# Layer 2's output projection in four parts, one of them by seven products of halves, and half of a gate's row sums moved to layer 1

## The chip, the cores and the metric

One core of a Trainium2 chip runs the whole program. Its engines work side by side, each through its own queue in program order: TensorE (PE) multiplies, VectorE (DVE) and ScalarE (ACT) work on elements, GpSimd (POOL) does a few small operations, and SyncE (SP) issues most of the transfers from HBM. An instruction waits until what it needs is there, and everything behind it in the same queue waits with it. The metric is the device time of one execution in microseconds (us); less is better.

## The reference

A two-layer trunk over 512 tokens of width 2048, in float32. Layer 1 mixes tokens by retention, layer 2 by latent attention; each ends in an output projection whose result is scaled by a gate and added to its input:

```python
x = x + gate1 * ((silu(g) * retention(q, k, v)) @ w_ret_out)      # layer 1
x = x + gate2 * ((silu(g) * attention(q, k, v)) @ w_mla_out)      # layer 2
out = rmsnorm(x, final_g)
```

The gates (and the shifts and scales of the two norms) are row sums of a large matrix with the conditioning vector: `mod = ada_w @ silu(c)`. `w_mla_out` is 2048 x 2048. This is a condensed form of the reference.

## The kernel before

**Products.** Float32 accuracy comes from three passes: each operand is split into a high and a low part (ACT casts, DVE subtracts), and PE adds hi x hi, hi x lo and lo x hi. So one block of a projection, 128 rows of input by 128 columns of weights over 512 tokens, takes three products of 128x512. A function `split` does the cast and the subtraction. For a weight tile of 128x1024 they are one instruction each.

**Seven products.** Some projections of the kernel are computed by halves (a form of Strassen's method, `seven_rows_steps`): rows of inputs and columns of weights are cut in two, sums and differences are formed, and seven products of halves replace eight. They run in two phases. Phase one has four steps of four products into banks x, s, z, y of PSUM; phase two has three products a step, which add onto x, y and s. Between the phases ACT copies x to m1 and s to m5 (L991), and DVE adds them into y (L1056) and s (L1058). Layer 2's gate is computed so (tiles `g_00e` to `g_13o`; "e" and "o" are the even and odd row halves, "10" to "13" the units of phase two).

**Layer 1's output projection** (L1486) runs in three blocks of sixteen steps and a last block. A step has one unit of weights: `o_n_r_u_r` as loaded, `o_n_r_u_p` its two split parts, 24 products of 128x512. Beside it run the heads of retention: statistics on DVE (L1320), a root on POOL (L131), `nmr` on DVE (L1326), the normalisation on ACT (L1332). Between them stand row sums for later modulations: a load of 512 KB by SP (L1165) into one of two buffers, and a sum on DVE (L1170) over 128x1024. How many sums each step gets is a list of step numbers given to `light`; the loads come one step ahead.

**Layer 2's output projection** takes the columns of `w_mla_out` in three rounds. Rounds 0 and 1 take a quarter each (512 columns; 8 units of 24 products, four banks). The last round takes the third and fourth quarter together (L2450): 16 units of 1024 columns, one row block each, into eight banks. Of them the last five units (`N_ENDS`) are held back and multiplied bank by bank in two halves of the tokens, so that outputs can start early. Inputs are loaded once, but split again in each round (`o2_parts`). In this stage also run the loads and sums for the second half of layer 2's gate (`gate_load`, `gate_sum`, L2157). An output (`o2_out`) is a DVE operation that scales by the gate and adds the residual (L2417), a square on ACT (L2422), a multiplication on ACT (L2423) and an addition of the squares on DVE (L2427).

**What sets the order.** The program is written out in order, and a scheduler places instructions of the engines within it; `behind(...)` and `queued(...)` pin a piece of code behind what was last placed on the named engines. Raw weights have three buffers (`raw`), split ones three pairs.

Of the kernel before, what the change touches and what calls it, by code (L numbers as in the profile page):

```python
# [16 lines left out]
P = 128  # L17
# [32 lines left out]
def hybrid_trunk_kernel(  # L50
# [1101 lines left out]
    row_pieces = [(0, 2, 0), (0, 2, 1), (1, 0, 0), (1, 0, 1), (1, 1, 0), (1, 1, 1)]  # L1152
# [397 lines left out]
    light(block, (0, 0, 2, 2, 4, 5, 6, 6))  # L1550
# [589 lines left out]
    gate_sums = [base.tile([P, 2, 8], F32, tag="mod_c", bufs=2, name=f"gate_sums{i}") for i in range(2)]  # L2140

    def gate_load(part, n):

        j, b = n // 8, n % 8
        if b == 0:
            half = gate_c_half[j] = big(f"c_gate{part}{j}", F32)
# [4 lines left out]
        aw = l2_tile("bw", 2, f"mod_gate_{part}{b}{j}", (P, 2, T))  # L2151
        r0 = 2 * D + (8 * part + b) * P
        nc.sync.dma_start(aw, ada_t[1, r0 : r0 + P, j * 1024 : (j + 1) * 1024].rearrange("p (a n) -> p a n", a=2))
        return aw, part, j, b, gate_c_half[j]

    def gate_sum(aw, part, j, b, c_half):
        DVE.scalar_tensor_tensor(  # L2157
            out=aw, in0=aw, scalar=1.0, in1=c_half, op0=ALU.mult, op1=ALU.mult,
            accum_out=gate_sums[part][:, j, b : b + 1],
        )  # L2160
        if (j, b) == (1, 7):
            use_modulation(1, 2, part, gate_sums[part])

    def attention_step(pr):
# [5 lines left out]
        with behind(S_):  # L2170
            sums = [gate_load(0, 2 * nx + i) for i in range(2)]
# [189 lines left out]
    x2 = [k4(f"x2_{j}", F32) for j in range(KD // 2)]  # L2361
    ss2 = l2p.tile([P, T], F32, tag="o2", bufs=2, name="x2_ss")
    o2_in, o2_res = {}, {}
    N_ENDS = 5

    gate_pending, gate_n = [], [0, 0]

    def o2_hooks(i):
        l2_hooks.get(i, lambda: None)()
        with behind(V_):  # L2370
            while gate_pending:
                gate_sum(*gate_pending.pop())
        with behind(S_):
            for _ in range(min(1, 16 - gate_n[0]) if 4 < i and i > gate_n[1] else 0):
                gate_pending.insert(0, gate_load(1, gate_n[0]))
                gate_n[0] += 1
        gate_n[1] = i

    def o2_parts(r, u):
        if u not in o2_in:  # L2380
            o2_in[u] = big(f"o2_in{u}", F32)
            nc.sync.dma_start(o2_in[u], o2_d[u * 2 * P : (u + 1) * 2 * P, :].rearrange("(k p) n -> p k n", p=P))
        own = big if (r, u) == (2, KD // 2 - 1) else k4b
        hi, lo = own(f"o2_h{r}_{u}"), own(f"o2_l{r}_{u}")
        split(o2_in[u], hi, lo)
        return hi, lo

    o2_split = {(0, 0): queued(o2_parts, 0, 0)}
# [4 lines left out]
    def o2_unit(r, u, kn, cn, where=None):  # L2393
        halved = kn == 1 and u >= KD - N_ENDS
        with ExitStack() as stack:
            for ins in o2_first if (r, u) in ((0, 1), (0, 2)) else ():
                stack.enter_context(tc.issue_after(ins))
            wt = load_w(
                [(whole, rows(w_mla_out, u, kn, r * T, cn))], kn, cn, f"o2_w{r}_{u}", where=where, halved=halved
            )  # L2400
        k = r, u * kn // 2
        if k not in o2_split:
            o2_split[k] = o2_parts(*k)
        return wt, o2_split[k]

    def o2_moving(w, kt, cols=slice(0, T)):
        return tuple(a[:, kt % 2, cols] for a in w[1])

    def o2_out(kt, ps, half=None):

        cols = slice(0, T) if half is None else slice(half * H, (half + 1) * H)
        if kt not in o2_res:
            tag, bufs = ("sg", 3) if kt >= 13 else ("pp", 5)
            o2_res[kt] = l2p.tile([P, T], F32, tag=tag, bufs=bufs, name=f"o2_xr{kt}")
            nc.sync.dma_start(o2_res[kt], x1_d[kt * P : (kt + 1) * P, :])
# [200 lines left out]
```

## Time and profile before

| | us |
|---|---|
| median of three runs (2119.68 to 2120.03) | 2119.76 |
| span of the profiled execution | 2118.4 |
| layer 1's output projection, PE | 997.2 to 1430 |
| layer 2's output projection, rounds 0 and 1, PE | 1920.7 to 2017.0 |
| the last round, PE (L2450) | 2017.0 to 2105.7 |

The profiled execution was not timed by itself; its span is 1.4 us under the median of the runs. The row of a timeline gives the start and the length of a piece of work in us, the engine, the line, the operation, what is written and read, and in brackets how long the engine had been idle before it and what ended that. Rows of the chain give start, length, engine and line. Names are without buffer numbers, so `o_p` is the split weights of any unit. Rows of matmuls give their full latency; the pace is the distance from start to start.

### The profile page before, as it was taken

How to read it: one execution, taken by the hardware profiler on the slowest of the kernel's cores; microseconds unless marked ns; L12 is line 12 of the kernel's file. 1: busy time of each engine (PE TensorE's matmuls, PEld its weight loads, DVE VectorE, ACT ScalarE, POOL GpSimd, SP SyncE). 2: the span in 40 equal slices, each digit the busy share in tenths (PEclk: the TensorE clock that was granted, in tenths of full speed). 3: DMA queues.
4: the chain of work that ended last, by engine and by line, in shares of the span. 5: the costliest groups of instructions: out<-in, count | busy, mean ns of one | idle time of the engine just before them, and what ended most of it. 6: DMA issues, size and time to landing. Idle time of an engine off the chain costs nothing.

```text
span 2118.4 us, 30062 instructions
## 1 busy us (share of the span) xinstructions
PE 2104.0 (99%) x11124; PEld 1812.6 (86%) x11124; DVE 1676.0 (79%) x2506; ACT 1055.5 (50%) x1622; POOL 103.6 (5%) x176
## 2 busy tenths in 40 slices
PE   8999999999999999999999999999999999999998
PEld 6888898989889888888888888898889989888888
DVE  7899888888888789666777778768978788886665
ACT  6765444444454444434344444345446575664443
POOL 1001010000000000000000000010001000000000
PEclk9999999999999999999999999999999999999999
DMA  9975786868787778856657556753566644346643
GB/s 381 406 280 195 248 276 222 283 211 272 239 263 250 242 229 283 265 172 196 222 173 241 201 198 230 258 191 108 164 189 209 190 129 149 118 137 219 222 142 138
DMA packets 230101, 462.95 MB, mean 219 GB/s; under 512 B 20881, under 2 KB 84401, under 8 KB 226369
## 3 DMA queue, kind: packets, MB, share of 16 engines
q1 hardware_dynamic: 217312, 421.07, 60.3%
q0 software_dynamic: 11920, 38.91, 4.7%
q8 instruction: 87, 1.43, 0.3%
q10 hardware_dynamic: 722, 1.06, 0.2%
q14 instruction: 60, 0.49, 0.1%
HBM read 417.96 MB, written 43.00 MB: 218 GB/s over the span
## 4 chain that ended last, share of the span: by engine, by line
PE 96%; DMA 1%; DVE 1%; ACT 0%; issue 0%; SPq 0%; DVEq 0%
PE o L1486 16%; PE o L2450 4%; PE x L884 2%; PE x L883 2%; PE x L885 2%; PE y L885 2%; PE y L884 2%; PE s L885 2%; PE s L884 2%; PE s L883 2%; PE y L883 2%; PE uv L2046 2%; PE qk L158 2%; PE s_qk L984 2%; PE x_qk L984 2%; PE qk L160 2%
## 5 line engine op out<-in xcount | busy, mean ns | idle before, releaser
L1486 PE MATMUL o<-o_h,o_p 128*128 128x512 f32 (+1 forms) x1088 | 323.0, 378 | 0.0
L1486 PEld LDWEIGHTS o<-o_h,o_p 128*128 128x128 f32 x1088 | 200.2, 188 | 37.1
L1486 PE MATMUL o<-o_l,o_p 128*128 128x512 f32 (+1 forms) x544 | 204.8, 376 | 0.0
L136 DVE TENSOR_TENSOR o_p<-o_r,o_p 128x1024 fp32r<-128x1024 f32 x64 | 78.1, 1222 | 54.3 <-ACT o_p L135 54.1
L1486 PEld LDWEIGHTS o<-o_l,o_p 128*128 128x128 f32 x544 | 102.3, 188 | 18.3
L2450 PE MATMUL o<-o_h,o_w 128*128 128x512 f32 (+1 forms) x336 | 82.7, 337 | 0.0
L1170 DVE SCALAR_TENSOR_TENSOR mod<-mod,c_odd 128x1024 f32<-128x1024 f32 x56 | 67.2, 1219 | 15.3 <-DMA mod<-in_ada_t_dram 15.3
L135 ACT CAST o_p<-o_r 128x1024 fp32r<-128x1024 f32 x64 | 66.7, 1054 | 22.4 <-PE o L1486 13.3
L158 PE MATMUL qk<-hT,qk_p 128*128 128x512 f32 x192 | 75.0, 391 | 0.0
L160 PE MATMUL qk<-hT,qk_p 128*128 128x512 f32 x192 | 74.9, 390 | 0.0
L389 DVE SCALAR_TENSOR_TENSOR aw<-aw,c_all 128x2048 f32<-128x2048 f32 (+1 forms) x37 | 73.2, 1997 | 2.1 <-DMA aw<-in_ada_t_dram 2.1
L159 PE MATMUL qk<-hT,qk_p 128*128 128x512 f32 x192 | 74.7, 389 | 0.0
L2450 PEld LDWEIGHTS o<-o_h,o_w 128*128 128x128 f32 x336 | 57.7, 188 | 6.9
L2450 PE MATMUL o<-o_l,o_w 128*128 128x512 f32 (+1 forms) x168 | 56.5, 337 | 0.0
L136 DVE TENSOR_TENSOR o_l<-o_in,o_h 128x1024 fp32r<-128x1024 f32 x24 | 29.3, 1222 | 34.2 <-ACT o_h L135 34.2
L1332 ACT ACTIVATE yn<-y,nmr,gn_r 128x512 f32<-128x512 f32 x32 | 22.3, 778 | 67.7 <-DVE nmr L1326 67.7
L135 ACT CAST o_h<-o_in 128x1024 fp32r<-128x1024 f32 x24 | 25.3, 1052 | 61.6 <-PE o L159 40.5
L158 PE MATMUL o<-o_h,o_w 128*128 128x512 f32 x128 | 50.1, 391 | 0.0
L160 PE MATMUL o<-o_h,o_w 128*128 128x512 f32 x128 | 49.8, 389 | 0.0
L159 PE MATMUL o<-o_l,o_w 128*128 128x512 f32 x128 | 49.8, 389 | 0.0
L1170 DVE SCALAR_TENSOR_TENSOR mod<-mod,c_bm 128x1024 f32<-128x1024 f32 x40 | 48.7, 1219 | 0.0
L448 PE MATMUL g<-hT,g_p 128*128 128x512 f32 x192 | 46.1, 389 | 0.0
(1532 smaller groups left out, 6238.3 us busy)
## 6 DMA issues: line engine op xcount, KB each, us to landing
mod<-in_ada_t_dram SPq DMA_DIRECT2D x96, 512.0 KB, 5.7
o_r<-in_ret_w_out_dram SPq DMA_DIRECT2D x64, 512.0 KB, 5.5
aw<-in_ada_t_dram SPq DMA_DIRECT2D x28, 1024.0 KB, 9.5
mod_gate<-in_ada_t_dram SPq DMA_DIRECT2D x32, 512.0 KB, 4.4
o_w_raw<-in_mla_w_out_dram SPq DMA_DIRECT2D x32, 512.0 KB, 4.4
qk_r<-in_ret_w_in_dram SPq DMA_DIRECT2D x48, 256.0 KB, 3.5
qk_r<-qk_d SPq DMA_DIRECT2D x32, 256.0 KB, 6.1
v_r<-v_d SPq DMA_DIRECT2D x32, 256.0 KB, 5.7
```

The source lines that it names most:

```text
L135: ACT.copy(hi, src)
L136: DVE.tensor_sub(lo, src, hi.bitcast(F32))
L158: PE.matmul(o, lhs[0], rhs[0], start=first and not seeded, stop=False, skip_group_check=seeded)
L159: PE.matmul(o, lhs[0], rhs[1], start=False, stop=False, skip_group_check=seeded)
L160: return PE.matmul(o, lhs[1], rhs[0], start=False, stop=last, skip_group_check=seeded)
L883: PE.matmul(banks[b], a[0], w[0], start=first, stop=False, skip_group_check=True)
L884: PE.matmul(banks[b], a[0], w[1], start=False, stop=False, skip_group_check=True)
L885: PE.matmul(banks[b], a[1], w[0], start=False, stop=True, skip_group_check=True)
L984: PE.matmul(o, w[wp][:, i, b * P : (b + 1) * P], a[ap], start=first and i + b + k == 0, stop=k == 2, skip_group_check=True,)
L1170: DVE.scalar_tensor_tensor(out=aw, in0=aw, scalar=1.0, in1=silu_c[j], op0=ALU.mult, op1=ALU.mult, accum_out=row_sums[piece][:, j, b : b + 1],)
L1486: PE.matmul(o, w[i][:, ki, c0 + b * P : c0 + (b + 1) * P], a[j], start=first and i + j == 0, stop=last and i == 1, skip_group_check=True,)
L2450: PE.matmul(banks2[b][:, cols], w[0][i][:, 0, b * P : (b + 1) * P], o2_moving(w, u, cols)[j], start=u + i + j == 0, stop=u == KD - 1 and i ...
```

## The change

Three things are changed.

1. The last round is cut in two. The third quarter is computed by seven products of halves (tiles `o_2_00e` to `o_2_13o`), in the banks of round 0. The fourth quarter takes eight units of two row blocks into four banks; the last five units are held back and multiplied in halves of the tokens, as before.
2. Inputs are split once (`o2_parts`, eight splits) and kept. New are sums and differences of the inputs' halves (`o2_sums`) and their splits, `o2_s` and `o2_t`, for the seven products. Outputs of round 1 and of the third quarter are kept in a list (`waiting`) and taken out one at a time by `put_one`.
3. The second half of layer 2's gate, 16 loads and 16 sums, is no longer in this stage. It joins the row sums of layer 1's projection as a seventh piece, with step numbers added to the lists.

The order of rows shows three places. The first is on DVE in step 13 of the first block of layer 1's projection. `mod_...` are the rows loaded, `o_0_3_3_p` is the split of that step's weights, `st` and `bn` are the head's statistics. Before:

```order
L136 TENSOR_TENSOR v_3_9571<-v_3_r,v_3_9571 128x512
L1170 SCALAR_TENSOR_TENSOR mod_0_1_21_9533,mod_0_1_c<-mod_0_1_21_9533,c_odd_8729 128x1024
L1170 SCALAR_TENSOR_TENSOR mod_0_1_30_9535,mod_0_1_c<-mod_0_1_30_9535,c_odd_8728 128x1024
L136 TENSOR_TENSOR o_0_3_3_p<-o_0_3_3_r,o_0_3_3_p 128x1024
L1320 BN_STATS st_0_9640<-y_0_9598 128x6
```

Now:

```order
L136 TENSOR_TENSOR v_3_9581<-v_3_r,v_3_9581 128x512
L1170 SCALAR_TENSOR_TENSOR mod_0_1_40_9541,mod_0_1_c<-mod_0_1_40_9541,c_odd_8727 128x1024
L1170 SCALAR_TENSOR_TENSOR mod_0_1_41_9543,mod_0_1_c<-mod_0_1_41_9543,c_odd_8728 128x1024
L1170 SCALAR_TENSOR_TENSOR mod_0_1_50_9545,mod_0_1_c<-mod_0_1_50_9545,c_odd_8727 128x1024
L136 TENSOR_TENSOR o_0_3_3_p<-o_0_3_3_r,o_0_3_3_p 128x1024
L1320 BN_STATS st_0_9651<-y_0_9608 128x6
```

Three sums stand in a row where there were two, and the sums are further along in the matrix. Steps 9 and 13 of the second block and 13 of the third look the same. SP's queue there, now:

```order
L1165 DMA mod_0_1_40_9541<-in_ada_t_dram 128x1024
L1165 DMA mod_0_1_41_9543<-in_ada_t_dram 128x1024
L1165 DMA mod_0_1_50_9545<-in_ada_t_dram 128x1024
L1472 DMA o_1_3_0_r<-in_ret_w_out_dram 128x2x512
L1272 DMA sg_0_9549<-g_d 128x512
```

The third load stands ahead of the next unit's weights and of the head's gates, where the second stood last.

The second place is ACT between the two phases of the seven products, first as layer 2's gate has it, before and now (`qT` belongs to other work):

```order
L1033 CAST g_10e<-g_10e_r 128x512
L1878 ACTIVATE qT_14756<-qT_14724,qn_s 128x512
L1878 ACTIVATE qT_14759<-qT_14729,qn_s 128x512
L1878 ACTIVATE qT_14762<-qT_14734,qn_s 128x512
L1878 ACTIVATE qT_14765<-qT_14739,qn_s 128x512
L991 COPY m_g_14816<-x_g_14548 128x512
L991 COPY m_g_14819<-s_g_14549 128x512
L1028 CAST g_11o<-g_11o_r 128x1024
L1033 CAST g_11e<-g_11e_r 128x512
```

and as the new third quarter has it:

```order
L1033 CAST o_2_10e<-o_2_10e_r 128x512
L135 CAST o_t_18889<-o_t6f 128x2x256
L135 CAST o_t_18892<-o_t7f 128x2x256
L1028 CAST o_2_11o<-o_2_11o_r 128x1024
L1033 CAST o_2_11e<-o_2_11e_r 128x512
L991 COPY m_o_2_18955<-x_o_2_18670 128x512
L991 COPY m_o_2_18958<-s_o_2_18671 128x512
```

In the new part the copies of x and s stand behind the casts of unit 11, and ahead of them in the gate.

The third place is DVE in the fourth quarter, now. `o_w_3` to `o_w_7` are its weights by unit, L2443 and L2455 the outputs' scaling and their squares' addition:

```order
L136 TENSOR_TENSOR o_w_3_19196<-o_w_3_r,o_w_3_19196 128x1024
L2443 SCALAR_TENSOR_TENSOR x_5_19229<-s_o_2_18671,gate_c_93,o_xr_19062 128x256
L2443 SCALAR_TENSOR_TENSOR x_5_19229<-m_o_2_18958,gate_c_93,o_xr_19062 128x256
L2455 TENSOR_TENSOR x_ss<-x_ss,x_sq_0_19232 128x512
L2443 SCALAR_TENSOR_TENSOR x_5_19229<-s_o_2_18671,gate_c_93,o_xr_19105 128x256
L2443 SCALAR_TENSOR_TENSOR x_5_19229<-m_o_2_18958,gate_c_93,o_xr_19105 128x256
L2455 TENSOR_TENSOR x_ss<-x_ss,x_sq_0_19238 128x512
L136 TENSOR_TENSOR o_w_4_1_19243<-o_w_4_r,o_w_4_0_19242 128x1024
L136 TENSOR_TENSOR o_w_6_19246<-o_w_6_r,o_w_6_19246 128x1024
L136 TENSOR_TENSOR o_w_5_1_19282<-o_w_5_r,o_w_5_0_19281 128x1024
L136 TENSOR_TENSOR o_w_7_19285<-o_w_7_r,o_w_7_19285 128x1024
```

Two of the third quarter's four outputs stand ahead of unit 3's split and two between those of units 3 and 4; before, no output stood between the last units' splits.

The diff, cut to what the steps above and below speak of:

```diff
-    row_pieces = [(0, 2, 0), (0, 2, 1), (1, 0, 0), (1, 0, 1), (1, 1, 0), (1, 1, 1)]
+    row_pieces = [(0, 2, 0), (0, 2, 1), (1, 0, 0), (1, 0, 1), (1, 1, 0), (1, 1, 1), (1, 2, 1)]
...
+    more_rows = ((3, 8, 8, 13), (3, 4, 8, 9, 13), (2, 5, 8, 8, 10, 13))
...
-        light(block, (0, 0, 2, 3, 4, 6, 6, 7, 9, 9, 11, 11, 12, 13, 13, 15))
+        light(block, (0, 0, 2, 3, 4, 6, 6, 7, 9, 9, 11, 11, 12, 13, 13, 15) + more_rows[n])
...
-    light(block, (0, 0, 2, 2, 4, 5, 6, 6))
+    light(block, (0, 0, 2, 2, 4, 5, 6, 6, 7))
...
+    with behind(V_, A_):
+        seven[1].units[0][1]()
+    for j, step in enumerate(seven):
+        with behind(S_):
+            if j + 3 < 8:
+                seven[j + 3].units[0][0]()
+            else:
+                last_load(j - 5)
+            if j > 3:
+                o2_residual(4 + j)
+        with behind(T_):
+            step.multiply()
+        with behind(V_, A_):
+            if j + 2 < 8:
+                seven[j + 2].units[0][1]()
+            elif j == 6:
+                n_pairs[0] = n_pairs[1]
+                last_prepare(0)
+            if 0 < j < 3:
+                o2_late_sums(2 * j + 2)
+                o2_late_sums(2 * j + 3)
+        with behind(V_, A_, T_):
+            step.follow()
+        if j < 3:
+            put_one()
+            put_one()
...
+    ahead = {0: (3,), 1: (4, 6), 2: (5, 7)}
+    with behind(V_, A_):
+        last_prepare(1)
+        last_prepare(2)
+    for u in range(8 - N_ENDS):
+        with behind(S_):
+            for n in ahead[u]:
+                last_load(n)
...
+        with behind(T_):
+            for b in range(4):
+                last_product(u, b)
+        put_one()
+        put_one()
+        with behind(V_, A_):
+            for n in ahead[u]:
+                last_prepare(n)
...
+    def o2_end(b, half, between={}):
+        for u in range(8 - N_ENDS, 8):
+            last_product(u, b, both_halves[half])
+            between.get(u, lambda: None)()
```

`step.units[0][0]` loads a step's weights and `[0][1]` forms and splits them; `step.follow` of phase one's last step makes the copies of x and s; `last_load` and `last_prepare` load and split a unit of the fourth quarter; `put_one` places one waiting output on DVE and ACT.

More of the change, by code (lines that the diff above doesn't have):

```diff
@@ L2170, in attention_step @@
         with behind(S_):
-            sums = [gate_load(0, 2 * nx + i) for i in range(2)]
+            sums = [gate_load(2 * nx + i) for i in range(2)]
         if here:
@@ L2373, in o2_hooks @@
[L2373 to L2386, printed above, removed]
@@ L2391, in hybrid_trunk_kernel, with o2_unit @@
         scored(last[0])
-    def o2_unit(r, u, kn, cn, where=None):
-        halved = kn == 1 and u >= KD - N_ENDS
+    def o2_unit(r, u):
         with ExitStack() as stack:
@@ L2455, in hybrid_trunk_kernel @@
[L2455 to L2468 removed]
+    last_raw, last_w = {}, {}
+    N_ENDS = 5
@@ new lines, in hybrid_trunk_kernel, with last_product @@
+    banks3 = [aux(f"o2_3_{b}") for b in range(4)]
+    def last_product(u, b, cols=slice(0, T)):
+        for ki in range(2):
+            for i, j in ((0, 0), (0, 1), (1, 0)):
+                PE.matmul(
+                    banks3[b][:, cols], last_w[u][i][:, ki, b * P : (b + 1) * P], o2_moving(2 * u + ki, cols)[j],
+                    start=u + ki + i + j == 0, stop=u == 7 and ki + i == 2, skip_group_check=True,
+                )
+    ahead = {0: (3,), 1: (4, 6), 2: (5, 7)}
+    with behind(V_, A_):
+        last_prepare(1)
+        last_prepare(2)
```

221 lines of the change are left out of this document (144 added, 77 removed).

## Prediction

> **What bounds the kernel now.** I read the page's table of busy time first, then the chain that ended last, then PE's waits, and then the timelines of the places that the change touches.
>
> ```profile
> span 2118.4 us, 30062 instructions
> PE 2104.0 (99%) x11124; PEld 1812.6 (86%) x11124; DVE 1676.0 (79%) x2506; ACT 1055.5 (50%) x1622; POOL 103.6 (5%) x176
> PE 96%; DMA 1%; DVE 1%; ACT 0%; issue 0%; SPq 0%; DVEq 0%
> PE c_ps L474 <- DMA c_all<-in_c_dram: 3.2, 1, 3.2
> PE xT_ps L474 <- DVE x_diag L571: 2.2, 3, 1.2
> ```
>
> PE is busy for 99% of the span and holds 96% of the chain. Its two longest waits are 3.2 and 2.2 us, at the start. So time changes in two ways only: PE gets less to do, or PE is made to wait where it never waited. DVE at 79% has room on average, so it matters only where one instruction of PE needs one of DVE in time.
>
> **PE's work, minus 5.4 us.** Two rows of the chain give the pace of both widths.
>
> ```profile
> 1004.43 32.68 PE o L1486 x144
> 1655.08 1.36 PE y_g L984 x12
> ```
>
> A 128x512 product takes 32.68/144 = 0.227 us, a 128x256 one 1.36/12 = 0.113. Quarters three and four now take 264 whole and 240 half products; 264 x 0.227 = 59.9. After, 336 products of 128x256 (4 steps of 48, 4 of 36) and 72 whole ones: 38.1 + 16.3 = 54.4, beside the same 240 halves. That is -5.4, and the sum stands on it. "Perfetto Trace Analysis", section Matmuls, of the Trainium skill holds that larger matmuls are more efficient, which speaks against trading 192 wide products for 336 narrow ones. The rows disagree: half the width takes half the time. By the fixed 2.5 ns per matmul of its page "TensorE: Matmul & The Clock Gate", Back-to-back issue gap, an estimate, 336 x 109 ns against 192 x 216 ns saves 4.7.
>
> **Row sums in layer 1's projection, plus 8.7 us.** The sixteen sums and their 512 KB loads move here. Loads use two buffers, so load k waits until DVE has ended sum k-2. Four steps (13 of block 0, 9 and 13 of block 1, 13 of block 2) now have three sums back to back: the third's load can be issued only when the first has ended. What that takes, the stage already shows:
>
> ```profile
> 1108.75 1.22 DVE L1170 SCALAR_TENSOR_TENSOR mod<-mod,c_odd 128x1024 f32<-128x1024 f32 x1
> 1111.03 1.22 DVE L1170 SCALAR_TENSOR_TENSOR mod<-mod,c_odd 128x1024 f32<-128x1024 f32 x1
> 1115.06 1.23 DVE L1170 SCALAR_TENSOR_TENSOR mod<-mod,c_odd 128x1024 f32<-128x1024 f32 x1 [2.81 <-DMA mod<-in_ada_t_dram]
> 1044.84 1.23 DVE L1170 SCALAR_TENSOR_TENSOR mod<-mod,c_odd 128x1024 f32<-128x1024 f32 x1 [2.29 <-DMA mod<-in_ada_t_dram]
> ```
>
> From the end of sum k-2 (1109.97) to sum k: 5.1 us, 2.28 of it covered by a sum and a split. The second such place waited 2.29 over the same work, 4.6 in all; I take 4.6, 4.1 to 5.1. In a triple the third sum so shifts DVE's queue by 4.6. Queued behind it:
>
> ```profile
> 1093.19 1.22 DVE L1170 SCALAR_TENSOR_TENSOR mod<-mod,c_odd 128x1024 f32<-128x1024 f32 x1
> 1094.33 1.22 DVE L1170 SCALAR_TENSOR_TENSOR mod<-mod,c_odd 128x1024 f32<-128x1024 f32 x1
> 1095.48 1.22 DVE L136 TENSOR_TENSOR o_p<-o_r,o_p 128x1024 fp32r<-128x1024 f32 x1
> 1101.25 0.16 DVE L1326 SCALAR_TENSOR_TENSOR nmr<-bn,gn_r 128x4 f32<-128x4 f32 x1 [1.12 <-POOL gn_r L131]
> 1101.45 2.79 ACT L1332 ACTIVATE yn<-y,nmr,gn_r 128x512 f32<-128x512 f32 x4 [9.06 <-DVE nmr L1326]
> 1104.11 2.01 ACT L135 CAST o_p<-o_r 128x1024 fp32r<-128x1024 f32 x2
> 1105.20 1.23 DVE L136 TENSOR_TENSOR o_p<-o_r,o_p 128x1024 fp32r<-128x1024 f32 x1 [3.79 <-ACT o_p L135]
> 1108.71 0.61 PE L1486 MATMUL o<-o_h,o_p 128*128 128x512 f32 x2
> ```
>
> The head's normalisation runs DVE, POOL, ACT in series, then ACT casts the next unit's weights (o_1_3_0) and DVE makes their lo half, ending 1106.43. PE starts that unit with the second product of the last row, 1108.94, and needs the lo half two products later, 1109.39: slack 2.96, stall 4.6 - 2.96 = 1.6. The other three:
>
> ```profile
> 1177.57 1.22 DVE L136 TENSOR_TENSOR o_p<-o_r,o_p 128x1024 fp32r<-128x1024 f32 x1
> 1181.11 0.61 PE L1486 MATMUL o<-o_h,o_p 128*128 128x512 f32 x2
> 1219.42 1.23 DVE L136 TENSOR_TENSOR o_p<-o_r,o_p 128x1024 fp32r<-128x1024 f32 x1 [3.79 <-ACT o_p L135]
> 1221.39 0.62 PE L1486 MATMUL o<-o_h,o_p 128*128 128x512 f32 x2
> 1330.71 1.23 DVE L136 TENSOR_TENSOR o_p<-o_r,o_p 128x1024 fp32r<-128x1024 f32 x1 [3.79 <-ACT o_p L135]
> 1333.56 0.62 PE L1486 MATMUL o<-o_h,o_p 128*128 128x512 f32 x2
> ```
>
> Slacks 3.0, 1.4, 2.3; stalls 1.6, 3.2, 2.3. Sum 8.7; with 4.1 or 5.1 it is 6.7 or 10.7. SP is moved past too: the next unit's raw weights and the gates stand behind the third load and leave when the first sum ends, some ten us before ACT's cast of them, against a 4 to 5 us wait; nothing. The other twelve sums bring waits like the two rows above, which cost PE nothing; nothing, and 1.2 each at worst where no idle time covers them. I take the small end, since DVE idles here for about 100 us of 433:
>
> ```profile
> 997.20:1430.00 432.80, 432.43 (x2119) 365.56 (x2118) 329.54 (x552) 189.27 (x293) 17.41 (x28) 1.00 0.63 216
> ```
>
> POOL's order is unchanged.
>
> **Between the two phases of the seven products, plus 4.2 us.** x's first product of phase two overwrites the bank that ACT copies to m1. In layer 2's gate, ACT copies before the eleventh unit's casts and PE runs on:
>
> ```profile
> 1613.89 0.62 ACT L1033 CAST g_10e<-g_10e_r 128x512 fp32r<-128x512 f32 x1 [1.57 <-PE y_g L984]
> 1615.21 0.59 ACT L991 COPY m_g<-x_g 128x512 f32<-128x512 f32 x1 [0.69 <-PE x_g L984]
> 1616.64 0.70 DVE L1056 TENSOR_TENSOR y_g<-y_g,m_g 128x512 f32<-128x512 f32 x1 [1.32 <-PE y_g L984]
> 1617.73 1.52 PE L984 MATMUL z_g<-h,g_03o 128*128 128x256 f32 x12
> 1619.09 1.52 PE L984 MATMUL x_g<-h,g_10o 128*128 128x256 f32 x12
> 1619.16 0.68 DVE L1030 TENSOR_TENSOR g_11e_r<-g_11o_r,g_11e_r 128x512 f32<-128x512 f32 x1
> 1619.76 1.22 DVE L1031 TENSOR_TENSOR g_11o<-g_11o_r,g_11o 128x1024 fp32r<-128x1024 f32 x1
> ```
>
> In the new order the copy stands behind the cast of 11e. That cast's buffer is read by z's product of step 03, PE's last of phase one. So PE must wait at least for cast and copy, 0.62 + 0.59, and 0.2 of hand-overs: 1.4. It also waits for DVE's subtraction of 11e. Phase one lasts 16 x 1.36 = 21.8 us. DVE's split of 02o ends at 7.7 (y of step 00 frees its pair at 5.4, cast and split follow). Behind it come four outputs, each output, square and sum 0.75 + 0.62 + 0.70 (the rows of the next part and L1056's), the third's wait filled (7.5); step 03, three subtractions and two splits, which follow each other at 0.60 and 1.14 us (4.1); step 10, 2.3; four splits of sums, 2.4: 24.0, and 11e's own 0.6. Cast and copy bring x to 25.9, 4.1 late; y's product needs two DVE additions of 0.70 against x's 1.36 and adds 0.1. I take 4.2; 1.4 to 5.5 (with a 1.05 cast of ACT in line).
>
> **The last quarter's weights, plus 4.2 us.** Raw weights have three buffers, so the load of unit 7 waits for DVE's split of unit 4, which stands behind four outputs.
>
> ```profile
> L2417 DVE SCALAR_TENSOR_TENSOR x<-o,gate_c,o_xr x24: 478/484/746, 1970.2 to 2106.0; 128x256 f32<-128x256 f32 x16, 128x512 f32<-128x512 f32 x8
> L2422 ACT ACTIVATE x_sq_None<-x x7: 615/617/633, 1972.8 to 2020.2; 128x512 f32<-128x512 f32 x7
> o_w_raw<-in_mla_w_out_dram SPq DMA_DIRECT2D x11, 512.0 KB, 4.1
> ```
>
> From the end of the seven products: two additions 1.4, splits of units 1 and 2 2.3, two outputs at 2.3 (two halves 0.9, square 0.62, sum 0.70, hand-overs) 8.3, unit 3's cast and split 10.4, two outputs 15.0, unit 4's 17.0. Then load 4.1, cast 1.0, hi 22.3, lo 23.5. PE needs unit 7's lo after 72 whole products (16.3), four units of six halves (2.7) and two more (0.2): 19.3. Wait 4.2, unit 5's share in it. If the outputs' four squares are filled by other work, 1.7; with a load as slow as the 5.1 us round above, 5.2.
>
> **The sum.** -5.4 + 8.7 + 4.2 + 4.2 = +11.7 on 2118.4, and the 1.4 us outside the span (2119.76 median): 2131.5. The rest costs nothing as I count it:
>
> ```profile
> 2017.00:2105.70 88.70, 88.70 (x513) 78.32 (x512) 51.69 (x79) 38.51 (x57) 0.72 (x1) 1.00 0.40 133
> ```
>
> Sixteen input splits and sixteen gate sums of 1.14 us leave the last stage (37 us of DVE). The sums of inputs come, 32 additions of half of 0.60 and 16 splits of 0.60 (about 20), and the third quarter's weights take 4 x 4.1 + 4 x 2.3 = 26 in place of eight splits of 1.14 (9). So DVE's load stays, and the 37 of 89 us that it idles there hide it; without that cover each split late for PE would cost its own 0.6 us. The tail behind PE's last product is built as before.
>
> **Rivals.** (1) Loads of the triples land under the slack and only the last stage waits: -5.4 + 8.4 = +3.0, 2122.8. For it: 100 us of idle DVE; against: the triples are back to back with a 5.1 us round. (2) Faster: DVE, rid of 32 operations of 1.2 us in the last stage, reaches 11e's subtraction and unit 4's split in time. It decides from 5.4 us of waits downward; with none, 2114.4. Against: the buffer of 11e alone holds PE 1.4 us. (3) The clock drops in a wait.
>
> ```profile
> 2111.00:2112.00 1.00, 0.13 (x2) 0.00 (x0) 1.00 (x2) 0.67 (x1) 0.00 (x0) 1.00 1.04 381
> 2114.00:2115.00 1.00, 0.00 (x0) 0.00 (x0) 0.00 (x0) 0.00 (x0) 0.00 (x0) 0.96 1.06 367
> 2115.00:2116.00 1.00, 0.00 (x0) 0.00 (x0) 0.00 (x0) 0.00 (x0) 0.00 (x0) 0.50 1.03 258
> ```
>
> PE's last product ends at 2111.1; the granted clock is 0.50 from 2114.9, 3.8 us of idle later, for the 3.5 us that are left. A wait of 4.2 us would meet it; 3.5 us at half pace lose 1.7: 2133.2, or 2134.9 for both late waits. "TensorE: Matmul & The Clock Gate", Part 1, of the Trainium skill has this rule, an idle window of about 3.4 us; the trace agrees at 3.8.
>
> **How the numbers follow.** The forecast 0.55, (1) 0.20, (2) 0.10, (3) 0.15. Bounds of the waits run from 9.8 to 21.4 us, 2124 to 2136. The range of 2117 to 2136 leaves out (2) and the top. A measurement tells 0.2%, 4.2 us: faster below 2115.5, slower above 2124.0. Faster 0.10, same 0.20 (all of (1)), slower 0.70.
>
> **What would show it.** In the changed profile: PE waits on o_p's lo at four places of the projection; before x's product of 10o a wait of about 4 us for the copy; before unit 7's first half product another, on ACT's cast; DVE waits of about 3.4 us on mod at the triples. It is wrong if PE's waits stay under 5 us, or if seven-product rows take more than 1.36.

## The result and the profile after

The changed kernel takes 2149.33 us (median of four runs, 2146.1 to 2150.92) beside 2119.9 us for the one before, measured on the same chip: a ratio of 1.0138, 95% interval 1.0123 to 1.0152. It is slower, by 1.4%. The forecast was 2131.5 with a range up to 2136: the direction was right, the loss was more than twice as large as forecast.

The page of the changed kernel, its span, busy times, and the chain's shares by engine (profiled execution 2146.1 us):

```profile
span 2144.3 us, 30401 instructions
PE 2107.9 (98%) x11268; PEld 1816.7 (85%) x11268; DVE 1697.3 (79%) x2562; ACT 1053.7 (49%) x1625; POOL 103.3 (5%) x176
PE 84%; DVE 8%; DMA 3%; ACT 2%; issue 2%; POOL 0%; SPq 0%; DVEq 0%; POOLq 0%; ACTq 0%
```

The span is 25.9 us longer. DVE has 21 us more to do, but its share of the span is the same 79%. What has changed is the chain: PE held 96% of it and now holds 84%, because the chain leaves PE wherever PE waits and follows the engines that it waits for.

PE's waits in the changed kernel, summed by what PE waited for (total, times, longest, in us):

```profile
PE o L1486 <- ACT o_p L135: 5.2, 3, 1.8
PE x_o L984 <- ACT m_o L991: 4.2, 1, 4.2
PE o L1486 <- DVE o_p L136: 3.3, 5, 1.0
...
PE yT L1345 <- DVE s_3f L1293: 1.9, 3, 0.8
PE o L2567 <- DVE o_w L136: 1.8, 2, 1.1
PE s L158 <- ACT yn L1332: 1.4, 1, 1.4
PE y L159 <- DVE v L136: 1.1, 2, 0.6
PE y L158 <- ACT v L135: 1.0, 1, 1.0
PE o L2567 <- ACT o_w L135: 1.0, 1, 1.0
```

None of these stood in the profile before. The rows on `o_p`, `yT`, `s` and `y` are layer 1's output projection with the heads of retention; `x_o` is the seam between the two phases of the seven products; `o_w` is the last quarter. To see how much each stage lost, take a product that both kernels have behind the first stage, the first of layer 2's gate by seven products. Its row in the timeline of PE, before:

```profile
1597.17 1.59 PE L984 MATMUL x_g<-h,g_00e 128*128 128x256 f32 x12
```

and after:

```profile
1618.27 1.59 PE L984 MATMUL x_g<-h,g_00e 128*128 128x256 f32 x12
```

So 21.1 of the 25.9 us are lost before 1618. The last round ran from 2017.0 to its last product's start at 2105.7, 88.7 us. Its first and last product in the timeline of after:

```profile
2038.07 0.28 PE L984 MATMUL x_o<-o_h,o_00e 128*128 128x256 f32 x1
...
2131.70 0.28 PE L2567 MATMUL o<-o_h,o_w 128*128 128x256 f32 x1
```

93.6 us, 4.9 more. Between these two stages both kernels take the same 419.8 us.

**The triples.** DVE in step 13 of the first block, after; the third sum is the one with the bracket:

```profile
1095.29 1.22 DVE L1170 SCALAR_TENSOR_TENSOR mod<-mod,c_odd 128x1024 f32<-128x1024 f32 x1
...
1096.43 1.22 DVE L1170 SCALAR_TENSOR_TENSOR mod<-mod,c_odd 128x1024 f32<-128x1024 f32 x1
...
1101.45 1.22 DVE L1170 SCALAR_TENSOR_TENSOR mod<-mod,c_odd 128x1024 f32<-128x1024 f32 x1 [3.79 <-DMA mod<-in_ada_t_dram]
...
1108.23 0.16 DVE L1326 SCALAR_TENSOR_TENSOR nmr<-bn,gn_r 128x4 f32<-128x4 f32 x1 [1.12 <-POOL gn_r L131]
1112.18 1.23 DVE L136 TENSOR_TENSOR o_p<-o_r,o_p 128x1024 fp32r<-128x1024 f32 x1 [3.78 <-ACT o_p L135]
```

SP's queue at that place, the third load:

```profile
1096.54 0.33 SPq L1165 DMA_DIRECT2D mod<-in_ada_t_dram  x1
```

The load left at 1096.54, right when the first sum had ended (1096.51), and the third sum began 4.94 us after that end. All that follows on DVE stands 4.9 us later than two sums would have put it, the lo half of the next unit's weights at 1112.18 among it. At the other three triples the third sum began 4.70, 4.22 and 4.74 us after the first one's end. PE, at the first triple:

```profile
1112.20 0.50 PE L1486 MATMUL o<-o_h,o_p 128*128 128x512 f32 x1 [1.74 <-ACT o_p L135]
...
1113.46 0.73 PE L1486 MATMUL o<-o_h,o_p 128*128 128x512 f32 x2 [0.52 <-DVE o_p L136]
```

These are the two products that the prediction named: the first of the new unit, and the one that needs the lo half. To find what a wait costs, each PE instruction's start was compared with that of the same instruction before; here the distance grows by 1.94 and 0.81 (an idle time in brackets is some 0.2 less than that, since a single product's row lasts 0.39 and its pace is 0.227). Over the four triples this growth is 2.75, 1.86, 2.93 and 2.67: 10.2 us. At the second triple it stands at two other products: the changed kernel has the products that need the lo half six places later in that unit, and the first of them, at 1190.03, grows by 1.29; the first product of the next column block, at 1199.82, waits for an ACT copy (L1434) behind the late cast, 0.57. Behind the triple of step 9 of the second block the next head's scores also wait for the late normalisation, 1.60 from start to start:

```profile
1195.41 0.50 PE L158 MATMUL s<-qk_0p,qk_0p 128*128 128x512 f32 x1 [1.44 <-ACT yn L1332]
```

That makes 11.8 us for the triples.

**Everywhere else in that stage.** Three other rows of PE's timeline:

```profile
1149.25 0.73 PE L1486 MATMUL o<-o_h,o_p 128*128 128x512 f32 x2 [0.99 <-DVE o_p L136]
...
1208.45 0.66 PE L1345 MATMUL yT<-ident,yn 128*128 128x128 f32 x4 [0.84 <-DVE s_3f L1293]
...
1298.36 1.20 PE L158 MATMUL y<-v,sT 128*128 128x512 f32 x4 [1.01 <-ACT v L135]
```

None is at a triple: they are another unit's weights, and the head's own products, whose scores and values pass through DVE. A clock drop behind the third triple takes 1.2 us (shown at the end). So 21.1 - 11.8 - 1.2 = 8.1 us lie in places that the prediction had at nothing. By the same growth, some 3.4 of them stand at the heads' transposes (`yT`), 3.2 at their value products (`y`) and 1.5 at units' weights (`o`).

### The profile page after: what moved, and what is told of

Same layout as the page of the kernel before. It is cut to its first block, busy times and chain, and to the rows that moved or that the text cites. A ratio compares the mean times of both kernels' runs of the same rounds, so it can differ in the third digit from the quotient of the medians.

```text
span 2144.3 us, 30401 instructions
## 1 busy us (share of the span) xinstructions
PE 2107.9 (98%) x11268; PEld 1816.7 (85%) x11268; DVE 1697.3 (79%) x2562; ACT 1053.7 (49%) x1625; POOL 103.3 (5%) x176
## 4 chain that ended last, share of the span: by engine, by line
PE 84%; DVE 8%; DMA 3%; ACT 2%; issue 2%; POOL 0%; SPq 0%; DVEq 0%; POOLq 0%; ACTq 0%
PE o L1486 7%; PE x L884 2%; PE x L883 2%; PE x L885 2%; PE y L885 2%; PE s L885 2%; PE y L884 2%; PE s L884 2%; PE s L883 2%; PE y L883 2%; PE uv L2047 2%; PE qk L158 2%; PE s_qk L984 2%; PE x_qk L984 2%; PE qk L160 2%; PE qk L448 2%
## 5 line engine op out<-in xcount | busy, mean ns | idle before, releaser
L1170 DVE SCALAR_TENSOR_TENSOR mod<-mod,c_odd 128x1024 f32<-128x1024 f32 x72 | 86.6, 1220 | 34.7 <-DMA mod<-in_ada_t_dram 34.7
L2567 PE MATMUL o<-o_h,o_w 128*128 128x256 f32 (+1 forms) x208 | 44.2, 307 | 2.8 <-DVE o_w L136 1.8
L2047 PE MATMUL uv<-ukv_p,kvT 128*128 128x256 f32 x384 | 46.1, 279 | 0.0
L136 DVE TENSOR_TENSOR qk_p<-qk_r,qk_p 128x1024 fp32r<-128x1024 f32 x23 | 27.9, 1222 | 22.6 <-ACT qk_p L135 22.3
L2047 PEld LDWEIGHTS uv<-ukv_p,kvT 128*128 128x128 f32 x384 | 44.9, 189 | 0.1
L160 PEld LDWEIGHTS qk<-hT,qk_p 128*128 128x128 f32 x192 | 36.0, 188 | 7.8 <-DVE qk_p L136 0.3
```

Source lines behind the costliest of these rows:

```text
L136: DVE.tensor_sub(lo, src, hi.bitcast(F32))
L160: return PE.matmul(o, lhs[1], rhs[0], start=False, stop=last, skip_group_check=seeded)
L1170: DVE.scalar_tensor_tensor(out=aw, in0=aw, scalar=1.0, in1=silu_c[j], op0=ALU.mult, op1=ALU.mult, accum_out=row_sums[piece][:, j, b : b + 1],)
L2047: PE.matmul(ps[:, (t % 2) * 256 : (t % 2 + 1) * 256], a[i], w[k], start=t % 2 + i + k == 0 and kt == 1, stop=kt == 3 and i == 1, skip_grou ...
```

## The experiments

The first seven kernels were run once each, the last three ten or eleven times. A stage's loss is read inside the profiled execution.

**One part alone.** `rows_alone` is the kernel before with the third part of the change only.

```diff
-    row_pieces = [(0, 2, 0), ..., (1, 1, 1)]
+    row_pieces = [(0, 2, 0), ..., (1, 1, 1), (1, 2, 1)]
+    more_rows = ((3, 8, 8, 13), (3, 4, 8, 9, 13), (2, 5, 8, 8, 10, 13))
...
-            for _ in range(min(1, 16 - gate_n[0]) if 4 < i and i > gate_n[1] else 0):
+            for _ in range(0):
```

> Only the third part of the change, on the kernel before: the sixteen row sums of the gate's second half run in layer 1's projection, by the change's step numbers; the last stage is that of before without them. If the loss of about 21 us that the changed kernel shows in layer 1's projection belongs to the rows there alone, that stage is again 20 to 22 us longer than before and the time is 2139 to 2145 us. If it depends on the seven products (their memory, their loads), less than half of it is here: under 2131.

2142.37 us (2120.13 for the kernel before on that chip). Its first product of layer 2's gate, in PE's timeline:

```profile
1619.19 1.60 PE L984 MATMUL x_g<-h,g_00e 128*128 128x256 f32 x12
```

It is 22.0 us later than before, with two clock drops where the changed kernel has one. The loss of the first stage belongs to the moved row sums and to nothing else in the change.

**Their place.** `spread` is the changed kernel with the same sixteen sums at other steps, so that no three stand together.

```diff
-    more_rows = ((3, 8, 8, 13), (3, 4, 8, 9, 13), (2, 5, 8, 8, 10, 13))
+    more_rows = ((1, 5, 8, 14), (1, 5, 8, 10, 14), (1, 5, 8, 8, 10, 14))
```

> The changed kernel with the same sums at other steps: (1, 5, 8, 14), (1, 5, 8, 10, 14) and (1, 5, 8, 8, 10, 14), so that no step has three. Buffer theory (the third sum in a row waits for a load that could only leave when the first had ended): the 14 us at the four triples go, 2 to 5 us stay at places with two sums and little between, so layer 1's projection is 3 to 7 us longer than before in place of 21, about 2133 in all. Work theory (sixteen more DVE operations of 1.15 us are too many for the stage): 15 us or more of the 21 stay, 2143 or more.

2129.89 us. DVE in step 13 of the first block of this kernel:

```profile
1094.40 1.22 DVE L1170 SCALAR_TENSOR_TENSOR mod<-mod,c_odd 128x1024 f32<-128x1024 f32 x1
...
1095.55 1.22 DVE L1170 SCALAR_TENSOR_TENSOR mod<-mod,c_odd 128x1024 f32<-128x1024 f32 x1
...
1102.47 0.16 DVE L1326 SCALAR_TENSOR_TENSOR nmr<-bn,gn_r 128x4 f32<-128x4 f32 x1 [1.12 <-POOL gn_r L131]
1102.55 1.22 DVE L1170 SCALAR_TENSOR_TENSOR mod<-mod,c_odd 128x1024 f32<-128x1024 f32 x1
...
1106.42 1.23 DVE L136 TENSOR_TENSOR o_p<-o_r,o_p 128x1024 fp32r<-128x1024 f32 x1 [2.64 <-ACT o_p L135]
```

The third sum now stands behind `nmr`, where DVE waits for ACT in any case: the wait for ACT's cast shrinks from 3.79 to 2.64, and the lo half at 1106.42 is 1.2 us later than before instead of 7. The first product of layer 2's gate:

```profile
1600.40 1.60 PE L984 MATMUL x_g<-h,g_00e 128*128 128x256 f32 x12
```

3.2 us of loss are left of 21.1, with the same number of loads and sums. That the loss is DVE's work as such falls with this: what costs is where the sums stand.

**The third loads alone.** `no_third_load` is the changed kernel without the loads of the four third sums; these four sums multiply the conditioning row by itself, so their results are left out of the modulation.

```diff
+            loaded = (piece, b, j) not in (((1, 0, 1), 5, 0), ((1, 1, 0), 4, 1), ((1, 1, 0), 7, 1), ((1, 2, 1), 2, 1))
+            if loaded:
                 nc.sync.dma_start(...)
...
-                    out=aw, in0=aw, scalar=1.0, in1=silu_c[j], op0=ALU.mult, op1=ALU.mult,
+                    out=aw, in0=aw if loaded else silu_c[j], scalar=1.0, in1=silu_c[j], op0=ALU.mult, op1=ALU.mult,
```

> The changed kernel, but at the four triples the third sum has no load: it multiplies the conditioning row by itself, so four of the row sums are wrong and four transfers of 512 KB are left out. The DVE work and its order are unchanged. Buffer theory: the 14 us at the triples fall to under 4, the 6 to 7 us elsewhere stay; about 2138. Work theory: nothing changes in the stage, 2147 to 2151. If SP's queue, held behind the waiting load, is what costs, it goes as well: this run parts load and work, not buffer and queue.

2138.19 us. Its first product of layer 2's gate:

```profile
1606.81 1.60 PE L984 MATMUL x_g<-h,g_00e 128*128 128x256 f32 x12
```

9.6 us of loss remain of 21.1, and 1.1 of them are a clock drop; without the drops of both runs the third loads are worth 19.9 - 8.5 = 11.4, beside the 11.8 read off above, and the wait of the scores is gone with them. The 8.5 stand with all four third loads gone: they are the other places. The largest of PE's waits there, in its sums of waits:

```profile
PE y L158 <- ACT v L135: 1.9, 1, 1.9
```

It is at the value products of the third block, where two sums were added to step 8, just ahead of the splits of the head's values on DVE.

**SP or the buffers.** `third_by_pool` has POOL issue the four third loads, so that SP is free for the weights and gates behind them.

```diff
-            nc.sync.dma_start(
+            third = (piece, b, j) in (((1, 0, 1), 5, 0), ((1, 1, 0), 4, 1), ((1, 1, 0), 7, 1), ((1, 2, 1), 2, 1))
+            (POOL if third else nc.sync).dma_start(
```

> The changed kernel, but the four third loads (block 0 step 13, block 1 steps 9 and 13, block 2 step 13) are issued by POOL, so that SP's queue (next weights, gates, values) is not held behind them; DVE still waits for each load. Buffer theory: DVE's wait of 3 to 4 us at the triples stays and with it PE's: layer 1's projection is 18 to 21 us longer than before. Queue theory (SP held up, and behind it the weights and values that ACT waits for): the loss at the second triple, 5.4 us, and part of the others goes; 10 to 15 us stay.

2157.57 us, slower by another 8, and a miss: layer 1's projection loses 28.9 us. DVE's waits on the row loads in this kernel:

```profile
DVE mod L1171 <- DMA mod<-in_ada_t_dram: 39.3, 16, 6.2
```

and in the changed one:

```profile
DVE mod L1170 <- DMA mod<-in_ada_t_dram: 34.7, 15, 3.8
```

The extra time is the clock: the granted clock halves four times there (at 1113, 1195, 1240 and 1362), which takes some 9 us, where the changed kernel has one drop of 1.2. Without the drops both lose about 20 us. So freeing SP gave nothing back. The waits got longer, not shorter (at the first triple POOL issued the load at 1097.05, SP at 1096.54), so the run doesn't say what SP's queue alone would be worth. The changed kernel's own trace speaks against it, at the first triple: the next unit's weights left SP at 1096.96, right behind the third load, and ACT cast them at 1111.10, behind the late normalisation. A third buffer for the row loads would test the buffers directly; it wasn't tried.

**The last round's two waits.** `last_stage_mended` is the changed kernel with the copies of x and s ahead of unit 11's casts, and with the third quarter's outputs behind the splits of the next units instead of ahead of them.

```diff
             step.multiply()
+        if j == 3:
+            with behind(V_, A_, T_):
+                step.follow()
...
-        put_one()
-        put_one()
         with behind(V_, A_):
             for n in ahead[u]:
                 last_prepare(n)
+        put_one()
+        put_one()
```

> The changed kernel with two pieces of the last stage in another order: the copies of x and s come ahead of unit 11's casts, and the waiting outputs of the fourth quarter's loop come behind the splits of the next units. Order theory: the 4.2 us wait for the copy and the half clock behind it go (under 1 us stays), and the three waits for units 5 and 7 go, so the time from the first seven product to PE's last product falls from 98.8 to 88 to 90 us, about 2139. Rival: DVE is late there anyway (its splits and outputs), and the waits move to the next thing that DVE makes; then 94 us or more stay.

2145.27 us; from the first of the seven products to PE's last instruction, the transposes of the tail among it, 97.4 us (98.8 in the changed kernel, 93.9 from the same round's start before), far from the 88 to 90 expected. The first four rows of PE's timeline in the last round that carry a wait:

```profile
2062.62 0.38 PE L984 MATMUL x_o<-o_h,o_10o 128*128 128x256 f32 x1 [1.53 <-ACT m_o L991]
2065.07 1.63 PE L984 MATMUL y_o<-o_t,o_10e 128*128 128x256 f32 x12 [0.76 <-DVE s_o L1058]
2077.19 0.50 PE L984 MATMUL x_o<-o_h,o_13o 128*128 128x256 f32 x2 [0.75 <-DVE o_13o L1031]
2100.81 0.38 PE L2571 MATMUL o<-o_h,o_w 128*128 128x256 f32 x1 [1.73 <-ACT o_w L135]
```

The 4.2 us before x's first product have become 1.5, but two waits on DVE have come behind it, and the last quarter waits 2.5 us (1.73 and another 0.76) where it waited 2.8. Moving the copies and the outputs as they are moved the waits. What the next run changes is how outputs follow each other: an output is a scaling on DVE, a square on ACT that waits for it, and an addition on DVE that waits for the square. Placed one after the other they leave DVE idle at each square, 4.9 us in this round (5.0 in the changed kernel).

**Outputs in pairs.** `mended_spread` joins `spread` with the copies moved, and places outputs two at a time: both scalings, then both additions, so that one's square is covered by the other's scaling. In the last quarter one pair stands behind unit 3's split and one ahead of unit 7's.

```diff
-    def put_one():
+    def put_two():
         if waiting:
-            with behind(V_, A_):
-                waiting.pop(0)()
+            late = [queued_out() for _ in range(2)]
+            for add in late:
+                with behind(V_, A_):
+                    add()
...
         for n in ahead[u]:
+            if n == 7:
+                put_two()
             with behind(V_, A_):
                 last_prepare(n)
+        if u == 0:
+            put_two()
```

> The changed kernel with the sums at the steps of the run with no triples, with the copies ahead of unit 11's casts, and with the waiting outputs taken in pairs (both outputs, then both additions of squares, so that DVE does not wait for each square) and placed between units 3 and 4 and before unit 7. Order theory of the last stage: from the first seven product to PE's last product 89 to 92 us (98.8 in the changed kernel, 93.9 for the same columns before), layer 1's projection 3 us longer than before: 2118 to 2121 us in all. Rival (DVE has too much to do in the last stage, whatever the order): 95 us or more stay, 2124 or more.

2122.31 us, 1.3 above the top of what was expected. Its last round's rows with a wait:

```profile
2043.25 0.39 PE L984 MATMUL x_o<-o_h,o_10o 128*128 128x256 f32 x1 [0.48 <-ACT m_o L991]
2045.69 1.68 PE L984 MATMUL y_o<-o_t,o_10e 128*128 128x256 f32 x12 [0.76 <-DVE s_o L1058]
2058.10 0.50 PE L984 MATMUL x_o<-o_h,o_13o 128*128 128x256 f32 x2 [0.61 <-DVE o_13o L1031]
```

The last quarter's waits are gone; in the seven products 1.9 us are left. DVE's waits for the squares fell to 1.9 us. The pairing and the new places came together, so what each of them is worth was not taken apart.

**Fewer sums per block.** `mended_spread2` moves three more of the sums into the short last block.

```diff
-    more_rows = ((1, 5, 8, 14), (1, 5, 8, 10, 14), (1, 5, 8, 8, 10, 14))
+    more_rows = ((1, 5, 8, 14), (1, 5, 8, 14), (1, 5, 8, 14))
-    light(block, (0, 0, 2, 2, 4, 5, 6, 6, 7))
+    light(block, (0, 0, 1, 2, 2, 3, 4, 5, 5, 6, 6, 7))
```

> The same, but each of the three blocks gets only the steps (1, 5, 8, 14) and the last block four more sums (steps 1, 3, 5, 7). If the 3 us that the spread sums still cost sit at steps 8 and 10 of blocks 1 and 2 (where the head's values and transposes wait for DVE), 1 to 2 us of them go: 2116 to 2119 us. If the last block has no room, PE waits there and nothing is won.

2129.41 us: a miss. In the last block, a row of DVE and two of PE's new waits:

```profile
1361.81 1.23 DVE L1170 SCALAR_TENSOR_TENSOR mod<-mod,c_odd 128x1024 f32<-128x1024 f32 x1 [4.11 <-DMA mod<-in_ada_t_dram]
...
1367.34 0.50 PE L1486 MATMUL o<-o_h,o_p 128*128 128x512 f32 x1 [0.95 <-ACT o_p L135]
...
1390.72 0.50 PE L1486 MATMUL o<-o_h,o_p 128*128 128x512 f32 x1 [1.15 <-ACT o L1434]
```

The sum of step 3 is the third behind the two of step 2 and waits 4.11 us for its load, as in the triples; the outputs behind it on DVE come late, and so do PE's next weights. The sums of steps 5, 5, 6, 6, 7 chain in the same way (waits of 1.27, 1.54 and 0.82).

**The best of these.** `mended_late` goes back to five, five and four sums in the blocks and two in the last, and moves a pair of outputs and the splits of four sums of inputs from phase one of the seven products into phase two.

```diff
+    more_rows = ((1, 5, 8, 10, 14), (1, 5, 8, 10, 14), (1, 5, 8, 14))
+    light(block, (0, 0, 1, 2, 2, 4, 5, 6, 6, 7))
...
-            if 0 < j < 3:
-                o2_late_sums(2 * j + 2)
-                o2_late_sums(2 * j + 3)
+            if 2 < j < 5:
+                o2_late_sums(2 * j - 2)
+                o2_late_sums(2 * j - 1)
...
-        if j < 3:
+        if j in (0, 4):
             put_two()
```

> The last stage mended further: the second pair of round 1's outputs and the splits of the input sums for phase two come after the copies, in phase two, where DVE has room; sums of rows at steps (1, 5, 8, 10, 14), (1, 5, 8, 10, 14), (1, 5, 8, 14), and one more in step 1 of the last block. Order theory: the seven products' two phases take 38.5 to 39.5 us (41.4 in the run before this, 44.5 in the changed kernel, 38.1 without any wait), layer 1's projection is 2.5 to 4 us longer than before, so 2117.0 to 2119.5 us, between 0.1% faster and the same. Rival (the outputs only move their wait into phase two): 41 us stay, 2120 to 2122, the same as or slower than before.

2120.43 us (11 runs) against 2119.92, ratio 1.0004, interval 0.9995 to 1.0013: no difference, and above the 2117.0 to 2119.5 expected, though the two phases take 38.9 us and layer 1 loses 3.1, both as expected. First and last product of its last round:

```profile
2020.08 0.28 PE L984 MATMUL x_o<-o_h,o_00e 128*128 128x256 f32 x1
...
2105.69 0.28 PE L2576 MATMUL o<-o_h,o_w 128*128 128x256 f32 x1
```

85.6 us, 3.1 less than before; and it starts 3.1 us later than before. One part gains what the other loses.

**The gain without the loss.** `no_moved_rows` is `mended_late` without the sixteen moved loads and sums at all.

```diff
-            use_modulation(1, 2, 0, gate_sums)
+            for part in range(2):
+                use_modulation(1, 2, part, gate_sums)
```

> This is mended_late without the sixteen loads and sums of the second half of layer 2's gate anywhere; the gate's second half takes the sums of its first half, so those sums are left out of the computation. If layer 1's projection loses its 3.1 us in mended_late to the moved sums alone, and the mended last round is 3.1 us shorter than before (85.6 against 88.7 us from its first product to PE's last of the outputs), this takes 2116.5 to 2117.5 us: the last round's gain by itself. If the loss in layer 1's projection had another cause, or the last round is shorter only because it starts later, it stays at 2119 to 2120.5.

2116.41 us (10 runs) against 2119.98, ratio 0.9983, interval 0.9973 to 0.9992, just under what was expected. The mended last round gains 0.17% where the moved sums cost nothing; this kernel only shows the size, since the sums have to be made somewhere.

**Another place for three of the sums.** `mended_early` is `mended_late` with one sum fewer in each block and three in the end of the projection ahead of it.

```diff
+    light(block, (13, 14, 15))
     n_p = len(steps)
...
-    more_rows = ((1, 5, 8, 10, 14), (1, 5, 8, 10, 14), (1, 5, 8, 14))
+    more_rows = ((1, 8, 10, 14), (1, 8, 10, 14), (1, 8, 14))
```

> This is mended_late with three of the moved sums taken out of layer 1's projection's blocks (one from the step 5 of each block) and placed in the last three steps of the projection ahead of it, where DVE idles. Theory: what layer 1's projection still loses (3.1 us) comes from row loads that are chained at the two buffers, above all at steps 5, 6, 6, 7; without step 5 it loses 0.5 to 1.5 us, and the kernel takes 2117.3 to 2119.0 us, faster than before by 0.04 to 0.12 per cent. Rival: each extra sum costs PE by its own work on DVE wherever it stands; then the loss stays at about 3 us and the time at 2120 to 2121 us.

2119.26 us (11 runs) against 2119.98, ratio 0.9996, interval 0.9987 to 1.0005: again no difference that can be measured. Its first product of layer 2's gate starts 2.7 us later than before, so taking step 5's sums out gave back 0.4 of the 3.1 us. The theory expected 1.6 to 2.6: it fell for this remainder. Its largest wait in the stage, in PE's timeline of the third block:

```profile
1312.85 0.66 PE L1345 MATMUL yT<-ident,yn 128*128 128x128 f32 x4 [0.84 <-DVE s_3f L1293]
```

The head's transposes wait for a score, as in `spread` and `mended_late`. Which of the remaining sums pushes them is not settled.

## Why the prediction was right in its direction and wrong in its size

**PE's work, -5.4: held.** In `no_moved_rows`, where 0.2 us of wait are left in it, the seven products take 38.9 us; 38.1 were worked out. The 0.8 us between stand in the sum below.

**The triples, +8.7: right in kind, 3.1 short.** 11.8 measured, 10.2 of it at products that wait for weights and 1.6 at a head's scores, which weren't named. The wait for the load was sized right: the third sum came 4.65 us after the first one's end on average, where 4.6 was taken. What was missed is that DVE came to three of the triples already late. Before the first triple, where no other triple stands ahead, its sums begin 2.1 us later than before (1095.29 against 1093.19) and PE runs only 1.4 us later: 0.7 us of the slack were gone. At the other three it was 0.7, 0.0 and 0.3. With that, the prediction's rule (time from the first sum's end to the third sum, less slack) gives 2.7, 2.4, 2.8 and 2.7, beside 2.75, 1.86, 2.93 and 2.67. At the first triple only the single sums ahead can have taken the slack, so part of this shortfall belongs to the next step.

**"The other twelve sums bring waits like the two rows above, which cost PE nothing; nothing, and 1.2 each at worst": this is the step that failed.** They cost 8.1 us, and `no_third_load` leaves 8.5 with all four third loads gone. The reason given was that DVE idles for about 100 of 433 us in the stage. That is an average over the stage. Some of that time stands behind `nmr`, where DVE waits 3.8 us for ACT's cast, as the prediction's own rows show, and none of the twelve sums was there; five of them stand at step 8, ahead of a head's scores and value splits, which go through DVE to PE. `spread` shows that the place decides: as many sums, with a third one behind `nmr` instead of ahead of the statistics and single ones at steps 1, 5 and 14, leave 3.2 us of loss in all. Four of its sums still stand at step 8, so that step alone doesn't explain the 8.1. The prediction read the slack of the weights at each triple, row by row; for the other twelve sums it read no row. What each of the twelve costs by itself was not taken apart.

**The seam, +4.2: held.** 4.2 us in PE's waits, for the copy, as worked out; phase one and the copy each ended some 0.8 us later than worked out, which cancels. **The last quarter's weights, +4.2: held roughly.** Three gaps, the first and the last of them in PE's timeline of the changed kernel:

```profile
2101.97 0.50 PE L2567 MATMUL o<-o_h,o_w 128*128 128x256 f32 x2 [1.09 <-DVE o_w L136]
...
2105.66 0.50 PE L2567 MATMUL o<-o_h,o_w 128*128 128x256 f32 x2 [0.76 <-DVE o_w L136]
```

With the one between (0.99, for ACT's cast) they are 2.8 us of idle time, 3.6 from start to start. `last_stage_mended` shows that the story behind both terms was too simple: each was told as one piece of code in the wrong place, and with that piece moved the wait came back in another. With the outputs in pairs and at other places the waits went; which of the two did it stays open.

**The third rival came to pass beside the forecast.** It was set against the forecast as another case, but it is an addition: the clock halved behind the wait at the seam. Granted clock (eighth column; before it busy times of PE, PEld, DVE, ACT and POOL) by the microsecond:

```profile
2064.00:2065.00 1.00, 0.19 (x1) 0.19 (x2) 1.00 (x2) 1.00 (x3) 0.00 (x0) 0.78 0.82 279
2065.00:2066.00 1.00, 1.00 (x5) 1.00 (x6) 0.91 (x2) 0.24 (x1) 0.00 (x0) 0.50 1.00 217
```

The last product of phase one ended at 2060.6, and the clock fell at about 2064.6, some 4 us later, as the row behind PE's last product had it (3.8); the 24 products that follow take 4.3 us instead of 2.7. The rule of "TensorE: Matmul & The Clock Gate", Part 1, of the Trainium skill (an idle window of about 3.4 us) agrees here.

The account of the span: -5.4 (work) + 11.8 (triples) + 8.1 (the other sums) + 4.4 (the seam, from start to start) + 3.6 (the last quarter) + 1.6 + 1.2 (clock) + 0.8 (the seven products' pace) = 26.1, beside 25.9 measured. Of the 14.2 us by which the forecast's +11.7 was short, 8.1 are the twelve sums, 3.1 the triples' size and 2.8 the clock.

The first two rivals fell: the triples were not covered (1), and DVE, though rid of 32 operations in the last stage, reached neither of the late pieces in time (2).

## What to carry to other kernels

Idle time of an engine covers a new instruction only if it stands at that instruction's place in the queue: read the rows around every place where work is inserted, not the stage's average. Where a stage has few buffers for a stream of loads, spread the loads evenly, and put the work on them where its engine waits for another one anyway; here that alone was worth 18 of 21 us with the same work. When a wait is cured by moving one piece, ask what the engine does next in a chain with another engine: two independent chains can be placed side by side so that each covers the other's wait. Here the waits went when that was done together with a move, and not by a move alone.

## What the runs showed of the hardware that was not expected

The clock also fell after a much shorter wait. The third triple in the changed kernel, in PE's timeline:

```profile
1234.85 0.58 PE L1486 MATMUL o<-o_h,o_p 128*128 128x512 f32 x1 [1.83 <-ACT o_p L135]
```

PE ran dry at 1233.0 and had work again at 1234.85; the clock fell at 1235.13, 2.1 us after the last dense product, and stayed at half for 3.4 us; five products then start 0.4 apart or more, and the loss is 1.2 us. The first triple waited 1.74 and 0.52 us and kept its full clock, while in `rows_alone` the same place with nearly the same waits (1.66 and 0.53) lost it. So the length of the wait alone, 3.8 us in the row of before, doesn't decide.

The kept traces show what does. In all twelve, every change of the granted clock, 58 in all, lies a whole number of 3.413 us from the first one of its trace, within 0.004 us (before: 22.54 and 2114.91, 613 of them; changed kernel: 1235.13 and 2064.57, 243). So the clock is set anew at the ends of fixed windows of that length, wherever the program's waits fall, and PE's work within one window decides. The window at the first and at the third triple of the changed kernel, and the one at the first triple of `rows_alone`, in the columns used above:

```profile
1108.84:1112.25 3.41, 1.67 (x9) 1.06 (x7) 0.07 (x1) 3.41 (x6) 0.00 (x0) 1.00 0.27 106
1231.72:1235.13 3.41, 1.58 (x7) 1.03 (x6) 0.30 (x1) 3.41 (x6) 0.00 (x0) 1.00 0.48 185
1109.86:1113.27 3.41, 1.37 (x5) 0.48 (x3) 1.13 (x1) 3.41 (x5) 0.00 (x0) 1.00 0.01 5
```

The first was followed by full clock, the other two by half. Over all traces, every window at full clock with less than 1.5 us of PE work was followed by half clock and none with more than 1.8 was; between the two both occur. Thus a window that is about half idle is enough, and a wait near 2 us costs a drop or not by where it falls. The Trainium skill, "TensorE: Matmul & The Clock Gate", Part 1, calls the activity window free-running, and these traces agree. Its rule of an idle window does not cover the half idle ones; here the measurement decides.

A drop costs little by itself, but it can come on top of any wait near 2 us or more, and in a kernel with many such waits it isn't the same in each execution: the four runs of the changed kernel spread over 4.8 us (2146.1 to 2150.92), with a mean granted clock of 0.997 in the shortest and 0.994 in the longest, where those of the kernel before agree within 0.5.
